# One more plain unit ahead of the block combinations, z stored raw there, filler at the mixers' seam, stores from ScalarE's queue: a two-layer decoder trunk on one core

## The chip, the core and the metric

The kernel runs on one core of a Trainium2 chip. The metric is the device time of one execution in microseconds. A measured kernel is run several times and the median counts; beside it stands one execution taken by the hardware profiler, and all rows below are from that one. Names used: TensorE (PE in the rows; PEld are its weight loads), VectorE (DVE), ScalarE (ACT), GpSimd (POOL) and SyncE (SP), which here only issues DMAs.

## The reference

Two layers over a residual stream x of 1024 tokens by 1024 channels, in float32:

```python
h = rms_norm(x, norm_pre[l])
u = h @ w_in[l]
(a_q, a_k, a_v, a_z, b_q, b_kv, b_kr, b_z, c_q, c_k, c_v, c_z, g) = jnp.split(u, split_points, axis=-1)
oa = diff_attention(...)      # 4 heads, then rms_norm per head
ob = mla_attention(...)       # 8 heads, low-rank queries and keys, rotary part
oc = sliding_window_attention(...)   # 8 heads, window 128, sinks
gates = jax.nn.sigmoid(g).reshape(B, S, N_BRANCHES, D_MODEL)
y = (gates[:, :, 0] * ((oa * jax.nn.silu(a_z)) @ w_br_a[l])
     + gates[:, :, 1] * ((ob * jax.nn.silu(b_z)) @ w_br_b[l])
     + gates[:, :, 2] * ((oc * jax.nn.silu(c_z)) @ w_br_c[l]))
x = x + rms_norm(y @ w_out[l], norm_post[l])
x = x + jax.nn.sigmoid(x @ w_ple_gate[l]) * (p[l] @ w_ple_proj[l])
```

Three attention mixers read the same normed input: a (differential), b (latent, with rotary parts), c (sliding window). Each has 512 output channels and a gate input z of the same width; silu(z) is z times its sigmoid. g holds three gates of 1024 channels, one per mixer.

## The kernel before

**Arithmetic.** Every matrix product runs on pairs: a value is split in a high part H (a rounding copy, on ScalarE) and a low part L (value minus H, on VectorE or GpSimd; `split`, lines 78 and 93), and a product is three matmuls, H·H, H·L and L·H. The normed, transposed input `hT` stays in SBUF in that form for a whole layer.

**Units.** A unit is 128 columns of u for all 1024 tokens: two halves of 512 tokens, each a `group` (line 305) of 8 K-tiles by 3 matmuls, 48 matmuls of 128x512 in all. Its weights come by one DMA (`wr`, two buffers, line 277), and are split into `wH` and `wL` (two buffers each). `z_unit` (line 434) evaluates the sigmoid of the result on ScalarE, multiplies on VectorE and stores silu(z) to the DRAM tensor `z_d`. `g_unit` (line 446) copies the result on ScalarE and stores it raw to `g_d`; its `wL` is made on GpSimd. Both use the tile `zs` (two buffers) and store from SyncE.

**Order of a layer.** `seven`, then the mixers c (`sw`), a (`da`) and b (`mla`), then `merge` and `tail`.

`seven` (line 459) first runs the four units of z for mixer a. Then VectorE makes four sets of block combinations T of `hT` (lines 479 to 500), each split again, so that `pair` (line 509) can compute two units with 7 block products in place of 8: all of z for b and c, and the first third of g. The first product of a pair goes to a bank that ScalarE copies to `p1`. The rest of g, 16 units per layer, are the **fillers**.

**Fillers.** The mixers alternate dependent steps on all engines, with TensorE waiting for softmax parts. `fill(n)` takes n steps from the front of the list of fillers; a step is 6 matmuls, and a unit is 8 of these and two steps of evacuation. In `sw` each call takes what it asks for, in `da` and `mla` a credit of 0.35 per call decides. The counts at the call sites are in `FILL`, the credits in `RATE`. `fill(n, True)` takes steps without the credit.

**Order on the engines.** The program is written in one order; a scheduler puts the instructions of each engine in a fixed order, by their place in the program, with a time model of its own. Work under `high_priority` comes earlier. `keep` pins an instruction to its place in the program.

**Trig.** In layer 0, between the two groups of 8 tiles of `sw`, `setup_trig` computes sines and cosines of the positions: some thirty small VectorE steps (lines 231 to 257), two sines on ScalarE, two transposes on TensorE (line 263), four copies and eight stores of `rope_d`, which `mla` loads into `tq`.

**Seam of da and mla.** At the end of `da` the remaining products of the last block run with filler between them; `square_sums` (line 835) sums the last squares on TensorE (line 840); then six small operations make the norm's scale out of `s0` and `ms` (lines 893 to 898). `mla` then loads its entry weight in four chunks (line 1053, tiles `wr`, split into `WH` and `WL`, 416 columns) and computes 8 tiles of 128 tokens in `mla_entry`; `rows_due` puts the transposed scale (`put_rows`, line 639) in DRAM behind the first tile. `s0` lies in the pool of `da`, whose memory the next pools take.

**Merge.** `merge` (line 1134) has to form the gated outputs: a block is 128 channels by 512 tokens. `gated` (line 1221) loads o, z and the row of scales `rb`; for mixer a VectorE multiplies o by weight and scale (line 1240) and by z (line 1241), and the result is split into `oH`, `oL`. The remaining fillers are drained meanwhile, two or so blocks per filler unit; just before the last one's matmuls the first load of `w_br_a` is written (line 277). Then come the products with `w_br_a`, 16 groups of 12 matmuls; the first needs the blocks of the first 512 tokens, the second those of the other half. For b and c GpSimd multiplies o by `rb` (line 1235), and VectorE by z (line 1243).

The list of fillers and the order of a layer are set in `build`:

```python
self.units = self.later(*[self.g_unit(l, bi, j) for bi in (1, 2) for j in range(KT)])
for b, mixer in (("c", self.sw), ("a", self.da), ("b", self.mla)):
    self.rate = RATE[b]
    mixer(l)
self.merge(l)
self.tail(l)
```

## Time and profile before

| | us |
|---|---|
| median of 3 runs | 2655.87 |
| lowest and highest | 2653.82, 2656.6 |
| the profiled execution | 2653.98 |
| its span | 2652.2 |
| TensorE busy in it | 2587.8 (98%) |
| VectorE busy | 1659.6 (63%) |
| ScalarE busy | 1265.6 (48%) |
| GpSimd busy | 452.6 (17%) |

The span goes from the first to the last instruction of the profile; the execution's own time is 1.8 us longer. The mean granted clock of TensorE over the span is 0.995 of full speed. In the rows a time stands first, then the duration, the engine, the line of the kernel, the operation with its output and inputs; the brackets hold how long the engine had been idle and what ended that.

### The profile page before, as it was taken

How to read it: one execution, taken by the hardware profiler on the slowest of the kernel's cores; microseconds unless marked ns; L12 is line 12 of the kernel's file. 1: busy time of each engine (PE TensorE's matmuls, PEld its weight loads, DVE VectorE, ACT ScalarE, POOL GpSimd, SP SyncE). 2: the span in 40 equal slices, each digit the busy share in tenths (PEclk: the TensorE clock that was granted, in tenths of full speed). 3: DMA queues.
4: the chain of work that ended last, by engine and by line, in shares of the span. 5: the costliest groups of instructions: out<-in, count | busy, mean ns of one | idle time of the engine just before them, and what ended most of it. 6: DMA issues, size and time to landing. Idle time of an engine off the chain costs nothing. (4 is left out here: it accounts for less than half of the span.)

```text
span 2652.2 us, 35930 instructions
## 1 busy us (share of the span) xinstructions
PE 2587.8 (98%) x12832; PEld 2120.4 (80%) x12832; DVE 1659.6 (63%) x3312; ACT 1265.6 (48%) x2761; POOL 452.6 (17%) x375
## 2 busy tenths in 40 slices
PE   8999999999999999999999999999999999999999
PEld 6778777888878878888877887888878788888887
DVE  7654565777378756755475536457764787577553
ACT  5433654555377733433443436545553777234332
POOL 2210000000010114234412001000000111251441
PEclk9999999999999999999999999999999999999999
DMA  6233123111110169453332331322111101894442
GB/s 197 86 116 109 46 69 104 53 52 48 51 31 23 53 210 290 148 177 115 116 96 90 114 99 50 94 68 60 51 53 40 29 22 54 267 280 148 137 118 96
DMA packets 296818, 269.21 MB, mean 102 GB/s; under 512 B 24272, under 2 KB 237456, under 8 KB 296512
## 3 DMA queue, kind: packets, MB, share of 16 engines
q1 hardware_dynamic: 295568, 262.19, 33.1%
q0 software_dynamic: 1072, 4.73, 0.6%
q8 instruction: 101, 1.65, 0.3%
q14 instruction: 77, 0.63, 0.1%
HBM read 194.93 MB, written 61.44 MB: 97 GB/s over the span
## 5 line engine op out<-in xcount | busy, mean ns | idle before, releaser
L305 PE MATMUL mm<-big,wH 128*128 128x512 f32 x3456 | 1106.5, 395 | 4.9 <-ACT zs L78 2.4
L305 PEld LDWEIGHTS mm<-big,wH 128*128 128x128 f32 x3456 | 638.9, 188 | 128.7 <-ACT zs L78 3.2
L305 PE MATMUL mm<-big,wL 128*128 128x512 f32 x1728 | 680.0, 394 | 2.3 <-POOL wL L93 1.9
L305 PEld LDWEIGHTS mm<-big,wL 128*128 128x128 f32 x1728 | 324.9, 188 | 65.7 <-POOL wL L93 2.8
L78 ACT CAST wH<-wr 128x1024 fp32r<-128x1024 f32 (+3 forms) x252 | 212.2, 852 | 334.4 <-PE mm L305 230.4
L93 DVE TENSOR_TENSOR wL<-wr,wH 128x1024 fp32r<-128x1024 f32 (+2 forms) x220 | 222.6, 1021 | 234.4 <-ACT wH L78 229.8
L793 ACT ACTIVATE e<-sc,st 128x512 f32<-128x512 f32 (+3 forms) x384 | 221.7, 582 | 99.5 <-DVE st L790 71.7
L787 DVE TENSOR_REDUCE st<-sc 128x1 f32<-128x512 f32 (+3 forms) x384 | 209.1, 551 | 7.2 <-PE sc L104 3.4
L93 POOL TENSOR_TENSOR wL<-wr,wH 128x1024 fp32r<-128x1024 f32 x32 | 77.4, 2423 | 501.7 <-ACT wH L78 336.6
L78 ACT CAST wtH<-tr 128x512 fp32r<-128x512 f32 x204 | 115.4, 590 | 82.5 <-PE tr L822 65.4
L93 DVE TENSOR_TENSOR wtL<-tr,wtH 128x512 fp32r<-128x512 f32 x204 | 136.3, 682 | 27.4 <-ACT wtH L78 26.9
L822 PE MATMUL tr<-cm,e 128*128 128x128 f32 x864 | 148.4, 275 | 1.0 <-DVE e L933 0.5
L544 PE MATMUL mm<-T,aH 128*128 128x512 f32 x384 | 121.5, 397 | 4.6 <-DVE po L583 3.9
L822 PEld LDWEIGHTS tr<-cm,e 128*128 128x128 f32 x864 | 106.1, 141 | 20.3 <-ACT e L793 7.0
L104 PE MATMUL sc<-kA,q 128*128 128x256 f32 (+3 forms) x320 | 104.6, 337 | 1.6 <-ACT e L735 0.8
L104 PE MATMUL sc<-kB,q 128*128 128x256 f32 (+3 forms) x320 | 99.6, 320 | 0.0
L544 PEld LDWEIGHTS mm<-T,aH 128*128 128x128 f32 x384 | 70.6, 188 | 26.3 <-DVE po L583 9.8
L544 PE MATMUL mm<-big,wH 128*128 128x512 f32 x256 | 82.9, 397 | 8.4 <-ACT po L78 8.4
L93 POOL TENSOR_TENSOR kL<-vT,kH 64x512 fp32r<-64x512 f32 x32 | 42.2, 1318 | 265.6 <-ACT kH L78 200.2
L379 POOL TENSOR_TENSOR acc<-acc,sq 128x512 f32<-128x512 f32 x36 | 56.8, 1577 | 176.2 <-ACT sq L378 176.2
L913 DVE TENSOR_TENSOR sc<-sc,dab 128x256 f32<-128x256 f32 (+1 forms) x128 | 52.4, 412 | 47.8 <-PE sc L104 46.6
L305 PE MATMUL mm<-WH,big 128*128 128x416 f32 x256 | 76.9, 370 | 3.6 <-ACT WH L78 2.7
(340 smaller groups left out, 5065.3 us busy)
## 6 DMA issues: line engine op xcount, KB each, us to landing
wr<-w_in SPq DMA_DIRECT2D x108, 512.0 KB, 3.8
sig<-g_d SPq DMA_DIRECT2D x48, 512.0 KB, 6.0
g_d<-zs SPq DMA_DIRECT2D x64, 256.0 KB, 2.2
wr<-w_out SPq DMA_DIRECT2D x32, 512.0 KB, 4.1
wr<-w_ple_gate SPq DMA_DIRECT2D x32, 512.0 KB, 4.0
kB<-kA SPq DMA_DIRECT2D x80, 128.0 KB, 2.3
x<-x SPq DMA_DIRECT2D x16, 512.0 KB, 6.1
g_d<-sg SPq DMA_DIRECT2D x32, 256.0 KB, 2.1
```

Source lines behind the costliest of these rows:

```text
L78: nc.scalar.copy(out, in_)
L93: (nc.vector if le == "v" else nc.gpsimd).tensor_tensor(L, src, h, ALU.subtract)
L104: self.nc.tensor.matmul(ps, w, x, start=i == 0, stop=i == n - 1)
L305: self.nc.tensor.matmul(ps, w, x, start=i == 0, stop=i == n - 1)
L379: (nc.gpsimd if eng == "g" else nc.vector).tensor_tensor(st, st, sq, ALU.add)
L544: nc.tensor.matmul(ps, w, x, start=start and not i, stop=i == 11, skip_group_check=True)
L787: nc.vector.tensor_reduce(st[:, c:c + 1], ps[:, :w], AX.X, ALU.max, negate=len(ch) == 1)
L793: nc.scalar.activation(e[:, k0:k0 + w], pss[c][:, :w], AF.Exp, bias=st[:, 0:1], accum_out=sums[:, c:c + 1])
L822: self.nc.tensor.transpose(tr[:, (2 * a + q) * P:(2 * a + q + 1) * P], ws[q][:, kt * P:(kt + 1) * P], self.ident)
L913: nc.vector.tensor_tensor(ps[:, a - k0:w], ps[:, a - k0:w], bias[:, h, a - n + 256:k0 + w - n + 256], ALU.add)
```

## The change

1. `z_unit` copies the product on ScalarE and stores raw z; no sigmoid, no multiplication. `gated` takes the sigmoid of a's z on ScalarE and multiplies it in on GpSimd, for each of the 8 blocks.
2. One unit of g (the first of the second third) runs after the four units of z in `seven`, with its low part made on VectorE; 15 units per layer are left as fillers.
3. `setup_trig` becomes a generator that stops behind the sines; what follows (transposes, copies, stores) runs ahead of the fifth tile of the second group of `sw`.
4. The stores of g units, of a's z and of a's o are issued from ScalarE's queue.
5. At the seam one filler step runs ahead of `square_sums`, its first matmul pinned; the six scale operations go into `rows_due`, which runs behind the second tile of `mla_entry`; the first filler matmul behind that place is pinned too; `s0` moves to the pool that lives through the layers.

```diff
@@ -255,6 +255,7 @@
         nc.scalar.activation(sn[:, 1], ang, AF.Sin)
         V.tensor_scalar(tr[:, 0], sn[:, 0], -MLA_SCALE, None, ALU.mult)
         V.tensor_scalar(tr[:, 1:3], sn, MLA_SCALE, None, ALU.mult)
+        yield
 
         self.cosT = self.cp.tile([P, 8, 2, 16], F32, name="cosT")
         self.sinT = self.cp.tile([P, 8, 2, 16], F32, name="sinT")
@@ -302,7 +303,10 @@
             terms += [(sH, mH), (sH, mL), (sL, mH)]
         n = len(terms)
         for i, (w, x) in enumerate(terms):
-            self.nc.tensor.matmul(ps, w, x, start=i == 0, stop=i == n - 1)
+            ins = self.nc.tensor.matmul(ps, w, x, start=i == 0, stop=i == n - 1)
+            if self.pin:
+                self.keep(ins)
+                self.pin = False
             if i % 6 == 5:
                 yield
 
@@ -435,22 +439,20 @@
         W = self.load_w(self.win(l, OFF[b + "z"] + j * P))
 
         def evac(hf, ps):
-            nc = self.nc
             st = self.zp.tile([P, 512], F32, tag="zs", bufs=2, name=self.uid("zs"))
-            nc.scalar.activation(st, ps, AF.Sigmoid)
-            nc.vector.tensor_tensor(st, ps, st, ALU.mult)
-            nc.sync.dma_start(self.z_d[l, b][j * P:(j + 1) * P, hf * 512:(hf + 1) * 512], st)
+            self.copy("a", st, ps)
+            self.nc.scalar.dma_start(self.z_d[l, b][j * P:(j + 1) * P, hf * 512:(hf + 1) * 512], st)
 
         yield from self.unit(W, KT, self.hT, evac)
 
-    def g_unit(self, l, bi, j):
-        W = self.load_w(self.win(l, OFF["g"] + bi * D + j * P), le="g")
+    def g_unit(self, l, bi, j, le="g"):
+        W = self.load_w(self.win(l, OFF["g"] + bi * D + j * P), le=le)
 
         def evac(hf, ps):
             st = self.zp.tile([P, 512], F32, tag="zs", bufs=2, name=self.uid("zs"))
             self.copy("a", st, ps)
             r0 = bi * D + j * P
-            self.nc.sync.dma_start(self.g_d[r0:r0 + P, hf * 512:(hf + 1) * 512], st)
+            self.nc.scalar.dma_start(self.g_d[r0:r0 + P, hf * 512:(hf + 1) * 512], st)
 
         yield from self.unit(W, KT, self.hT, evac)
 
@@ -461,7 +463,7 @@
         with ExitStack() as ctx:
             z = [self.z_unit(l, "a", j) for j in range(4)]
             self.by_halves(*z[0:2])
-            self.drain(*z[2:4])
+            self.drain(*z[2:4], self.g_unit(l, 1, 0, le="v"))
             pl = self.pool("seven", ctx)
             T = [[None] * 4 for _ in range(4)]
 
@@ -690,8 +692,11 @@
                     if not l:
                         self.setup_vecs()
                         self.setup_lambda(pl)
-                        self.setup_trig(pl)
+                        trig = self.setup_trig(pl)
+                        next(trig)
                 for i in range(8):
+                    if g and i == 4 and not l:
+                        next(trig, None)
                     t = self.sw_tile(l, pl, g, i, bias, sink, qs, kA[g], kB[g], Vp)
                     next(t)
                     self.fill(FILL[0])
@@ -851,7 +856,7 @@
             nc.sync.dma_start(bias, self.bias_ap(0, 4))
             heads = []
             self.diag_tiles(pl)
-            s0 = pl.tile([P, 4, 8], F32, name=self.uid("s0"))
+            s0 = self.zp.tile([P, 4, 8], F32, tag="s0", name=self.uid("s0"))
             ms = self.zp.tile([P, 4, 8], F32, tag="ms", name=self.uid("ms"))
             self.s0, self.ms = s0, ms
 
@@ -886,17 +891,24 @@
                         nxt = self.later(*prep(h + 1), front=True)
                 self.drain(*nxt)
             self.weave(late, FILL[1], True)
+            self.pin = True
+            self.fill(1, True)
             self.square_sums(self.psum("av"))
 
             f = lambda t: t.rearrange("p h i -> p (h i)")
             s0, ms = f(s0), f(ms)
-            nc.vector.reciprocal(s0, s0)
-            nc.vector.tensor_tensor(ms, ms, s0, ALU.mult)
-            nc.vector.tensor_tensor(ms, ms, s0, ALU.mult)
-            nc.scalar.activation(ms, ms, AF.Sqrt, bias=self.eps, scale=1.0 / P)
-            nc.vector.reciprocal(ms, ms)
-            nc.vector.tensor_tensor(ms, ms, s0, ALU.mult)
-            self.rows_due = lambda: self.put_rows(pl, l, "a", ms)
+
+            def scale():
+                nc.vector.reciprocal(s0, s0)
+                nc.vector.tensor_tensor(ms, ms, s0, ALU.mult)
+                nc.vector.tensor_tensor(ms, ms, s0, ALU.mult)
+                nc.scalar.activation(ms, ms, AF.Sqrt, bias=self.eps, scale=1.0 / P)
+                nc.vector.reciprocal(ms, ms)
+                nc.vector.tensor_tensor(ms, ms, s0, ALU.mult)
+                self.put_rows(pl, l, "a", ms)
+
+            self.rows_due = scale
+            self.pin = True
             self.fill(FILL[6], True)
 
     def da_block(self, l, pl, h, b, t, bias, late):
@@ -948,7 +960,7 @@
             sq = pl.tile([P, 256], F32, tag="sq", bufs=2, name=self.uid("sq"))
             nc.scalar.activation(sq, av[:, :256], AF.Square)
             self.squares = sq, self.ms[:, h, 2 * b:2 * b + 2]
-            nc.sync.dma_start(self.o_d[l, "a"][h * P:(h + 1) * P, b * 256:(b + 1) * 256], o)
+            nc.scalar.dma_start(self.o_d[l, "a"][h * P:(h + 1) * P, b * 256:(b + 1) * 256], o)
 
         return rest()
 
@@ -1063,7 +1075,7 @@
                 self.weave(self.group(ps[:, :N], KT,
                                       lambda kt: tuple(x[:, sl] for x in self.hT[hf][kt]),
                                       lambda kt: (WH[:, kt], WL[:, kt])), 1, not hf and t < 2)
-                if self.rows_due:
+                if self.rows_due and t:
                     self.rows_due()
                     self.rows_due = None
                 r = p2.tile([P, 512], F32, tag="raw", bufs=5, name=self.uid("raw"))
@@ -1231,7 +1243,11 @@
                 rb[a * P // ns:(a + 1) * P // ns],
                 rd[j * ns + a:j * ns + a + 1, src[1]].to_broadcast([P // ns, 512]))
         nc.sync.dma_start(z, self.z_d[l, b][src])
-        if b != "a":
+        if b == "a":
+            sg = pl.tile([P, 512], F32, tag="sg", bufs=2, name=self.uid("sg"))
+            nc.scalar.activation(sg, z, AF.Sigmoid)
+            nc.gpsimd.tensor_tensor(z, sg, z, ALU.mult)
+        else:
             nc.gpsimd.tensor_tensor(o, o, rb, ALU.mult)
         yield
         if b not in og:
@@ -1357,13 +1373,14 @@
         self.setup()
         self.fillers, self.squares = [], None
         self.credit, self.rate, self.units = 0.0, 1.0, ()
+        self.pin, self.rows_due = False, None
         with self.ent:
             self.entry()
             self.setup_bias(self.pe)
         self.zp = self.pool("zst")
         for l in range(DEPTH):
             self.seven(l)
-            self.units = self.later(*[self.g_unit(l, bi, j) for bi in (1, 2) for j in range(KT)])
+            self.units = self.later(*[self.g_unit(l, n // KT, n % KT) for n in range(KT + 1, 3 * KT)])
             for b, mixer in (("c", self.sw), ("a", self.da), ("b", self.mla)):
                 self.rate = RATE[b]
                 mixer(l)
```

## Rows read from the trace of the kernel before

**Rows 1.** The page's first part: busy time, share of the span, instructions.

```profile
PE 2587.8 (98%) x12832; PEld 2120.4 (80%) x12832; DVE 1659.6 (63%) x3312; ACT 1265.6 (48%) x2761; POOL 452.6 (17%) x375
```

**Rows 2.** Waits of TensorE: waiting line, releaser, total us, times, longest us.

```profile
PE mm L544 <- ACT po L78: 8.4, 2, 7.5
PE mm L305 <- ACT zs L78: 4.4, 6, 1.2
PE tr L263 <- ACT sincos L252: 4.2, 1, 4.2
...
PE mm L305 <- ACT WH L78: 2.7, 2, 2.0
PE tr L639 <- DVE ms L898: 2.2, 1, 2.2
```

**Rows 3.** Windows: length, busy time (instructions) by engine, PE clock, DMA share, GB/s.

```profile
core 0: us, PE busy (x) PEld busy (x) DVE busy (x) ACT busy (x) POOL busy (x), PEclk, DMA share, GB/s
349.00:362.00 13.00, 8.85 (x39) 7.47 (x38) 9.49 (x37) 2.96 (x6) 0.00 (x0) 0.74 0.16 44
660.00:700.00 40.00, 36.77 (x183) 32.21 (x182) 14.35 (x29) 12.86 (x27) 5.67 (x3) 0.96 0.27 82
1389.00:1402.00 13.00, 5.53 (x18) 4.12 (x17) 11.64 (x20) 5.13 (x9) 0.00 (x0) 0.74 0.15 40
1970.00:2005.00 35.00, 30.42 (x146) 25.41 (x145) 16.11 (x30) 13.97 (x29) 5.66 (x3) 0.90 0.29 86
2258.80:2302.00 43.20, 43.20 (x193) 35.68 (x191) 23.87 (x29) 12.41 (x20) 9.46 (x5) 1.00 0.85 278
```

**Rows 4.** Timeline of TensorE at layer 1's first pair.

```profile
1397.02 1.22 PE L544 MATMUL mm<-big,wH 128*128 128x512 f32 x2 [7.47 <-ACT po L78]
...
1401.41 0.63 PE L544 MATMUL mm<-T,aH 128*128 128x512 f32 x2
```

**Rows 5.** Timeline of ScalarE at the same place.

```profile
1395.86 0.62 ACT L78 CAST T<-po 128x512 fp32r<-128x512 f32 x1 [4.35 <-DVE po L500]
1396.39 0.58 ACT L78 COPY po<-mm 128x512 f32<-128x512 f32 x1
```

**Rows 6.** Tile zs: its instructions, ns min/median/max, first and last start.

```profile
L453 SPq DMA_DIRECT2D g_d<-zs x64: 319/338/1365, 321.4 to 2305.8; - x64
L440 ACT ACTIVATE zs<-mm x16: 583/592/600, 32.8 to 1381.7; 128x512 f32<-128x512 f32 x16
L441 DVE TENSOR_TENSOR zs<-mm,zs x16: 678/682/691, 33.5 to 1383.5; 128x512 f32<-128x512 f32 x16
```

**Rows 7.** Timeline of ScalarE and SyncE at layer 0's seam.

```profile
667.76 1.68 ACT L78 CAST WH<-wr 128x832 fp32r<-128x832 f32 x2 [0.77 <-DVE ms L898]
...
670.65 0.34 SPq L453 DMA_DIRECT2D g_d<-zs  x1
...
672.04 0.91 SPq L1053 DMA_DIRECT2D wr<-w_in  x2
...
675.75 0.89 ACT L78 CAST WH<-wr 128x832 fp32r<-128x832 f32 x1 [5.12 <-DMA wr<-w_in]
```

**Rows 8.** Timeline of layer 1's merge prelude: SyncE, GpSimd and VectorE.

```profile
2260.30 0.39 SPq L277 DMA_DIRECT2D wr<-w_in  x1
...
2270.76 2.55 POOL L93 TENSOR_TENSOR wL<-wr,wH 128x1024 fp32r<-128x1024 f32 x1 [10.49 <-ACT wH L78]
2271.09 2.77 DVE L1241 TENSOR_TENSOR o<-o,z 128x512 f32<-128x512 f32 x1
...
2293.23 0.69 DVE L93 TENSOR_TENSOR oL<-o,oH 128x512 fp32r<-128x512 f32 x1 [0.69 <-ACT oH L78]
...
2293.66 0.39 SPq L277 DMA_DIRECT2D wr<-w_br_a  x1
...
2300.83 1.23 DVE L93 TENSOR_TENSOR wL<-wr,wH 128x1024 fp32r<-128x1024 f32 x1 [3.59 <-ACT wH L78]
```

**Rows 9.** GpSimd's multiplication in the pairs, ns min/median/max, first and last start.

```profile
L557 POOL TENSOR_TENSOR sg<-po,sg x32: 1284/1294/1695, 82.2 to 1472.2; 128x512 f32<-128x512 f32 x32
```

## The prediction, made before the change was run

> **What bounds the kernel now.** I read the page's busy table first: TensorE is busy 98% of the span [rows 1]. So only its gaps can be won, and the next view is the list of what TensorE waited for [rows 2]. Five entries there belong to places that the change touches: 8.4 us for the copy of p1 in the block combinations, 4.4 for the copies of z and g, 4.2 for the sine table, 2.7 for the chunks of the latent mixer's weight, 2.2 for the scale of the differential mixer. They make 21.9 us. The rest of what TensorE loses there doesn't show as waiting: after a gap the granted clock is low. The table of windows puts it at 0.74 around the trig gap and around layer 1's combinations, 0.96 and 0.90 at the two seams between the mixers [rows 3]. One minus the clock, times the length, gives 3.4, 3.4, 1.6 and 3.5 us, but part of that lies in the gap itself, so these are upper bounds. The timeline shows the rest of it: two matmuls take 1.22 us at 1397.02 and 0.63 us at 1401.41 [rows 4], 1.2 GHz against 2.4 GHz.
>
> The last window to read is the prelude of the merge, 2258.8 to 2302.0: TensorE has no gap there [rows 3], because four filler units cover what VectorE does. That cover is what the change spends.
>
> **Sum base.** Durations are those of the profiled execution: 2653.98 us, span 2652.2 and 1.8 around it. The median of the three runs, 2655.87, stands 1.9 above, so what I add up is taken off the median. Some 0.2%, 5.3 us, is what a measurement of this kernel can tell from no change.
>
> **A. A fifth unit ahead of the combinations, z stored raw.** In layer 1 TensorE ends its work at 1389.55 and waits 7.47 us for p1's copy on ScalarE [rows 4]. That copy stands behind a split of T, which itself waited 4.35 us for VectorE [rows 5]: VectorE's chain of combinations is late, and ScalarE's queue is in order. A unit is 48 matmuls; the prelude runs 193 in 43.2 us, 0.224 each [rows 3], so a unit covers 10.7 us. Eight multiplications of z per layer leave VectorE at 0.68 us each, 5.4 us [rows 6]; the unit's own wL split comes to VectorE at about 1.2, as that of w_br_a at 2300.83 does [rows 8]. Cover grows by 10.7, VectorE's load shrinks by some 4: the 7.47 goes whole, and so does its slow stretch, at most 3.4, of which I take 1.5. Layer 0 has only 8.4 − 7.47 = 0.9 us of this wait; I take it whole. That is 9.9, and **A = −9**, since a wait may come up at a later product of the pair; bounds −6 and −12. What is late next: the pair's products that take the splits of T in order.
>
> **B. The trig tail moves behind four tiles of the second group.** TensorE's transpose waits 4.2 us for the sine [rows 2], because VectorE works through the angle's many small steps first: it is busy 9.49 of that window's 13 us, in 37 instructions [rows 3]. Later transposes and filler come ahead of it now. Removed: 4.15 plus a slow stretch of at most 3.4, of which I take 2.6. But those 9.5 us of VectorE stay in front of the tiles' maxima, and only about 6 us of matmuls (two tiles' score products, transposes, three filler steps) can run meanwhile; so I take **B = −5** of the 6.75, bounds 0 and −6.75. The eight stores of rope_d move too, on SP, by four tiles; their reader is the latent mixer, whose weights in layer 0 are loaded at 672 [rows 7], 300 us later, so they cost nothing.
>
> **C. The seam, both layers.** Layer 1: 2.21 for the scale and 0.67 for the chunk, layer 0: 2.0 for the chunk [rows 2]; 4.9 us. The pinned filler step (6 matmuls, 1.4 us) stands where TensorE idled; the chain of six scale operations leaves the seam, and runs behind the second tile of the entry. Moving s0 to the longer-lived pool frees the memory of the mixer without waiting for the chain: in layer 0 the first cast of WH starts at 667.76, released by that chain [rows 7]. Slow stretches: at most 1.6 and 3.5, I take 1.4 and 2.1. Sum 4.9 + 3.5 = 8.4, **C = −8**, bounds −2 and −10. The new delay is that the rows' store goes out some 5 us later; its reader is the merge, whose blocks stand at 2271 in layer 1 [rows 8], over 260 us on: no cost.
>
> **D. Stores issued from ScalarE.** 112 stores leave SP: 64 of g, 16 of z, 32 of o. In layer 0's seam SP holds a store of g until its copy is done (670.65), and the loads of the last two chunks, written behind it, go at 672.04; their cast starts at 675.75 after 5.12 us of waiting [rows 7]. With the store on ScalarE's queue the loads can leave up to 2 us earlier; that is inside C. Elsewhere the z waits of 4.4 us lose their multiplication (0.68 of a chain of 0.59 + 0.68 [rows 6]) and one store's turn: **D = −1**, bounds 0 and −4.4.
>
> By the Trainium skill, "DMA: Bandwidth & Descriptors", section "Issuing engines are not separate DMA queues", DMAs begun from different engines share the same 16 DMA engines, and beginning them elsewhere saves only the sequencer's time. By that the chunk's 2.0 us at layer 0's seam would stay, and the sum would be 2 us worse. The order on SP [rows 7] is my reason not to take it: what is saved there is the turn behind a waiting store, not the issue.
>
> **E. What ScalarE pays.** No row has a DMA issued by ScalarE. Nearest: SP takes 0.34 us for one [rows 6]. 112 × 0.34 = 38 us of ScalarE's time, which is busy 48% of the span [rows 1]. Below: nothing, since a store follows a copy on the same engine (a gain is counted in D). Above: in the differential mixer (32 stores of o) ScalarE feeds the exponentials; if every one of those came late by 0.34, 11 us. The store also makes ScalarE's queue wait for nothing new: the copy ahead of it is its own. I take **E = +2**, nearer the lower end because TensorE's waits for ScalarE in that mixer are too short to stand among the first rows [rows 2].
>
> **F. The merge's prelude.** One unit fewer is left for it: cover falls from 43.2 to 32.5 us in layer 1. Needed by then: w_br_a's wL and the eight gated blocks, the second group of products (12 matmuls, 2.7 us in) needing the last four. Now the eighth block's oL ends at 2293.92, 35.1 after the mixer [rows 8]. w_br_a's load went out at 2293.66, and its wL ended at 2302.06, just as TensorE arrived [rows 8]. The load of the last filler unit, though, went out at 2260.30 [rows 8], as soon as its slot fell free: with one unit fewer w_br_a is that tile, and I expect it out there. The blocks: z now passes ScalarE (0.59 [rows 6]) and GpSimd (1.29 per multiplication [rows 9]) ahead of VectorE's o·z: 2 us at the start, and while GpSimd multiplies, VectorE's two-operand work stands, as it did for 2.77 in place of 0.69 beside the split at 2270.76 [rows 8]. Part of it falls in the 0.7 us that VectorE waits for each oH anyway; one filler split fewer on GpSimd gives back 2.1. So the eighth block at about 38 to 41 against 35 needed: **F = +4 per layer, +8**; bounds 0 and +15 per layer.
>
> **Sum.** −9 − 5 − 8 − 1 + 2 + 8 = −13: own time 2641.0, against the median **2642.9**, say 2643.
>
> **Rivals.**
> 1. *The merge starves (slower).* If w_br_a's load stays behind the blocks' loads on SP, as at 2293.66, all 10.7 us of lost cover per layer are stall, and blocks held by GpSimd add up to 8 × 1.29 = 10.3 less 2.1; I take 4. That is 15 per layer, 30 in all, in place of 8: −21 + 30 = +9, 2665. It decides from the point where the load leaves later than some 24 us after the mixer (33 less 8.4 for landing, cast and split). For it: the wL ended within 0.1 us of its use. Against: the slot falls free earlier.
> By the Trainium skill, "SBUF — State Buffer", section "SBUF: two separate sides", VectorE and GpSimd share one port pair as an exclusive lock held for the whole instruction. The rows agree (2.77 beside 2.55), and by the rule each of the 8 multiplications could hold VectorE fully.
> 2. *The gaps at trig and seams are only replaced*, VectorE's backlog and the chunks' landing being what they are: B 0, C −2, A −9, D 0, E +2, F +4 gives −5, about 2651, between 2649 and 2657.
> 3. *The change doesn't do what it says.* Only the first matmul of a filler step is pinned; a scheduler orders the rest by its own clock, and may pull the moved work back to where it was: with A partly filled and F paid, within 2651 to 2661.
> 4. *More than that*: F and E hidden, all gaps and slow stretches gone: −31 near the lower bounds, 2624.
>
> **Numbers.** Forecast (2630 to 2650) 0.57; more 0.10; replaced 0.13, of which 0.04 still faster by over 0.2%; not done 0.05; starved 0.15, of which 0.03 within 0.2%. Faster 0.57 + 0.10 + 0.04 = 0.71; same 0.09 + 0.05 + 0.03 = 0.17; slower 0.12. The range 2630 to 2660 leaves out the 0.10 below and about as much of the starved case.
>
> **What would show it.** A: no TensorE gap over 1 us at the first pair of layer 1, clock 1.00 there. B: no wait of L263's transposes, and waits of the scores for VectorE of no more than 2 us behind it. C: filler matmuls between the mixer's last products and the square sums; the scale chain after the second entry tile. D: loads of chunks leaving SP without a store between. E: no TensorE wait for ScalarE's exponentials that was not there. F: the first product with oH some 33 to 38 us after the mixer's end, and w_br_a's load before the blocks' loads. The prediction is wrong if TensorE stands over 10 us in either prelude, or if the seven's wait returns at a later pair.

## The result, and the profile after

The changed kernel takes 2669.78 us (median of 6 runs), the kernel before 2654.16 beside it: ratio 1.0055, 95% interval 1.0042 to 1.0068. It is 15.6 us slower, where 13 us faster was forecast. The profiled execution took 2670.93 us, its span is 2669.1. The page's busy times (the lines of the changed kernel lie up to 16 further down):

```profile
PE 2594.1 (97%) x12832; PEld 2127.3 (80%) x12832; DVE 1669.5 (63%) x3298; ACT 1279.3 (48%) x2779; POOL 470.4 (18%) x389
```

TensorE runs the same 12832 matmuls in 6.3 us more than before and stands 10.6 us longer; together these are the 16.9 us by which the span grew.

What TensorE waited for, total us, times, longest us:

```profile
PE mm L306 <- ACT zs L78: 10.9, 7, 2.9
PE sc L306 <- ACT oH L78: 5.2, 2, 2.8
PE mm L306 <- DVE wL L93: 4.7, 5, 2.1
PE sc L104 <- ACT e L798: 3.6, 5, 1.7
PE mm L306 <- ACT WH L78: 3.1, 2, 1.6
PE av L104 <- ACT wtH L78: 2.8, 3, 2.4
...
PE tr L641 <- DVE ms L907: 1.1, 2, 0.6
```

Against [rows 2], the waits for p1 (8.4) and for the sines (4.2) are gone, and that for the scale is half. In their place TensorE waits 10.9 us for the fillers' copies, 5.2 for gated blocks (`oH`), and the chunks (`WH`) cost 3.1, not less than before. The windows at the places of [rows 3], where each now lies:

```profile
335.00:348.00 13.00, 10.56 (x49) 8.64 (x48) 6.39 (x30) 6.87 (x24) 3.53 (x4) 0.87 0.48 94
660.00:700.00 40.00, 35.93 (x158) 29.85 (x158) 14.85 (x25) 13.19 (x25) 5.63 (x3) 0.83 0.27 82
1406.00:1419.00 13.00, 13.00 (x59) 10.76 (x58) 7.65 (x10) 6.68 (x10) 1.50 (x1) 1.00 0.20 61
1985.00:2020.00 35.00, 29.21 (x131) 23.21 (x130) 13.83 (x21) 12.31 (x21) 5.66 (x3) 0.85 0.29 86
957.30:1000.50 43.20, 35.62 (x144) 27.59 (x141) 29.08 (x28) 15.92 (x26) 15.30 (x11) 0.91 0.74 244
2277.50:2320.70 43.20, 38.30 (x164) 30.93 (x163) 25.37 (x27) 15.81 (x26) 15.96 (x12) 0.96 0.78 255
```

Layer 1's first pair runs without a gap at clock 1.00 (0.74 before). The trig part now costs a shorter gap (one wait of 2.4 us, clock 0.87). But the seams' clock went down, from 0.96 and 0.90 to 0.83 and 0.85, and in the 43.2 us after the latent mixer, where TensorE had one gap of 1.2 us in layer 0 and none in layer 1, it now idles 7.6 and 4.9 us.

Where the 16.9 us of span came from, by stretches between TensorE instructions that both traces have (last product with T; last sum of squares; last product with `WH`; transposition of the latent mixer's sums; last product with `og`, the gated blocks of mixer b, so that "merge" here ends with the products of b), in us:

| stretch | layer 0 before, after | layer 1 before, after |
|---|---|---|
| z units and pairs | 225.9, 230.3 | 469.9, 468.8 (with layer 0's tail) |
| mixers c and a | 439.9, 437.5 | 436.9, 434.6 |
| entry of the latent mixer | 61.0, 67.1 | 61.9, 66.8 |
| latent mixer | 215.9, 222.3 | 214.7, 217.2 |
| merge | 132.8, 132.9 | 131.3, 131.2 |
| tail | | 262.1, 260.5 |

The first row holds one more unit (10.7 us) in each layer, so it gained 6 in layer 0 and 12 in layer 1. The merge holds one unit less and takes as long as before: what was moved out of it, 10.7 us per layer, was lost there. The entry lost 11 us, where C had a gain of 8, and the mixer behind it 9, which no step of the prediction has (layer 0's holds 14 more matmuls than before, some 3 us of filler).

### The profile page after: what moved, and what is told of

Its sections match the earlier page's. It is cut to its first block, busy times and chain, and to the rows that moved or that the text cites. A ratio compares the mean times of both kernels' runs of the same rounds, so it can differ in the third digit from the quotient of the medians.

```text
span 2669.1 us, 35887 instructions
## 1 busy us (share of the span) xinstructions
PE 2594.1 (97%) x12832; PEld 2127.3 (80%) x12832; DVE 1669.5 (63%) x3298; ACT 1279.3 (48%) x2779; POOL 470.4 (18%) x389
## 4 chain that ended last, share of the span: by engine, by line
PE 82%; DVE 5%; DMA 5%; ACT 4%; issue 2%; SPq 1%; POOL 1%; ACTq 0%; DVEq 0%; POOLq 0%
PE mm L306 46%; PE sc L104 8%; PE mm L546 7%; PE av L811 5%; PE sc L306 4%; PE tr L827 3%; PE sc L546 2%; PE tr L306 2%; DMA wr<-w_in 2%; DMA wr<-w_br_b 1%; DVE wL L93 1%; ACT wH L78 1%; PE tr L748 1%; DVE o L1256 1%; ACT e L740 1%
## 5 line engine op out<-in xcount | busy, mean ns | idle before, releaser
L306 PE MATMUL mm<-big,wH 128*128 128x512 f32 x3456 | 1112.8, 397 | 10.6 <-ACT zs L78 8.0
L559 POOL TENSOR_TENSOR sg<-po,sg 128x512 f32<-128x512 f32 x32 | 44.6, 1393 | 215.5 <-ACT sg L557 215.5
```

The source lines that it names most:

```text
L306: ins = self.nc.tensor.matmul(ps, w, x, start=i == 0, stop=i == n - 1)
L559: nc.gpsimd.tensor_tensor(sg, src, sg, ALU.mult)
```

## The experiments

All ratios are to the kernel before on the same chip, with 95% intervals; 0.1% is 2.7 us.

**First four: one part undone in the changed kernel.** Silu back in the seven, and no sigmoid or GpSimd multiplication in the merge:

```diff
-            self.copy("a", st, ps)
+            nc.scalar.activation(st, ps, AF.Sigmoid)
+            nc.vector.tensor_tensor(st, ps, st, ALU.mult)
...
-        if b == "a":
-            sg = pl.tile([P, 512], F32, tag="sg", bufs=2, name=self.uid("sg"))
-            nc.scalar.activation(sg, z, AF.Sigmoid)
-            nc.gpsimd.tensor_tensor(z, sg, z, ALU.mult)
-        else:
+        if b != "a":
```

> The changed kernel with part 1 undone: z of the differential mixer gets its sigmoid and multiplication in the seven again, the merge does neither; the fifth unit, the seam, the trig split and ScalarE's stores stay. Theory M (the merge starves: GpSimd's eight multiplications stretch VectorE's chain of blocks, and one unit of cover is gone): the blocks' cadence goes back from 4.0 to 2.8 us, the eighth is done some 10 us earlier, and 15 to 25 of the 27 us lost in the merge come back: 2645 to 2655. Theory Q (ScalarE's queue, jammed by the stores it issues, makes the loss): within 4 us of the changed kernel, 2666 to 2674. Theory S (the seam with the moved scale chain makes it): the same, 2666 to 2674.

Measured: 1.0012 (1.0001 to 1.0023), 11 us faster than the changed kernel, less than theory M has and more than Q and S. The seven kept most of its gain (no wait for p1; its two stretches are 1.6 and 0.9 us longer), so with the unit ahead, raw z buys little there. Layer 1's merge fell to 122.7 us; in layer 0 it stayed at 131.3, now waiting for the casts of w_br_a's later loads.

The 112 stores back on SyncE (`nc.scalar.dma_start` to `nc.sync.dma_start` for g, z and o):

> The changed kernel with the 112 stores issued by SyncE again, all else as changed. Theory Q: the entry of the latent mixer and the mixer itself lost 17 us over both layers because casts and copies stand behind stores on ScalarE; most of it comes back, 2652 to 2660. Theory M: nothing in the merge depends on it, 2666 to 2674. Theory S: the entry's loss stays, 2666 to 2674; the chunk loads wait behind a store again, up to 2 us worse.

Measured: 1.0086 (1.0070 to 1.0101), 8 us slower still, which none of the three theories has. The entries took 71.5 and 68.6 us. Theory Q falls here: among the other parts, ScalarE's stores helped.

The seam as before:

```diff
-            self.pin = True
-            self.fill(1, True)
...
-            self.rows_due = scale
-            self.pin = True
...
-            s0 = self.zp.tile([P, 4, 8], F32, tag="s0", name=self.uid("s0"))
+            s0 = pl.tile([P, 4, 8], F32, name=self.uid("s0"))
```

> The changed kernel with the seam as before: no filler step ahead of the square sums, no pins, the scale chain at once, s0 in the mixer's own pool. Theory S: the entry took 10.5 us more in both layers together because the transposed scale stands in the middle of the first tiles and holds TensorE and the chunk casts; that comes back and the old gaps of 4.9 with it: 2661 to 2666. Theories M and Q: the seam had gained what was planned and the entry lost for other reasons, so undoing it costs 3 to 8 us: 2672 to 2678.

Measured: 1.0026 (1.0017 to 1.0035), 8 us faster. The entries went back to 61.3 and 63.1 us, as theory S has it: the seam, planned as a gain of 8, was a loss.

16 fillers and no fifth unit, z still raw:

```diff
-            self.drain(*z[2:4], self.g_unit(l, 1, 0, le="v"))
+            self.drain(*z[2:4])
...
-            self.units = self.later(*[self.g_unit(l, n // KT, n % KT) for n in range(KT + 1, 3 * KT)])
+            self.units = self.later(*[self.g_unit(l, n // KT, n % KT) for n in range(KT, 3 * KT)])
```

> The changed kernel with 16 filler units again and no fifth unit ahead of the combinations; z stays raw there and the merge's GpSimd multiplies. Theory M, cover part: TensorE has 10.7 us more per layer to run in the merge's prelude, so 15 to 21 us come back there; plain z alone must hold the seven's wait: if VectorE's 5.4 us are enough, the wait of 7.5 falls to 2, else it stays; 2650 to 2660. Theories Q and S: the merge's loss has nothing to do with cover; 2666 to 2676.

Measured: 1.0097 (1.0082 to 1.0112), 11 us slower than the changed kernel. The merges took 137.1 and 140.8 us: with a whole unit more to run, TensorE stood for the fillers' own copies (7.1 and 6.6 us). So what the merge lacks there is not cover. In layer 1 the wait for p1 fell from 7.5 to 2.3 us with raw z alone.

**Second four: pairs of parts.** The first run has units and z as before, the second also the seam, the third adds the unit to the second; the fourth is the changed kernel with the six scale operations in place and only `put_rows` deferred, behind the first tile.

> The changed kernel with the fifth unit and the raw z both undone (16 filler units, silu in the seven); trig split, seam and ScalarE's stores stay. Theory M2 (the merge takes the time that its blocks, weights and transfers need, some 131 us from the mixer's end to its last product, with or without the unit; each half alone left a loss there of 21 to 23 us of stalls against 4 before): with both undone the merge loses under 6 us in both layers together, the seven's wait of 7.5 is back, the seam's loss of some 6 stays: 0 to 5 us above the kernel before. Theory Q2 (the stores on ScalarE hold up casts in the merge): the stalls of 10 us or more in the merge stay without the multiplications, 8 to 20 us above the kernel before.

> The kernel before with only the trig split and the stores from ScalarE. Theory M2 with S: these two are the parts that gain outside the merge: trig 5, the stores some 2 to 5 at the seams; 4 to 10 us below the kernel before. Theory Q2: the stores cost 5 or more in the merge, so no better than the kernel before, minus 2 to plus 6.

> As the run with the trig split and the stores alone, with the fifth unit ahead of the combinations added (silu made in the seven, merge without sigmoid and multiplication, seam as before). Theory M2: the unit gains some 12 us in the seven and gives back what the merge cannot shorten by, 2 to 11 of it per layer: between 8 below and 2 above the run without it. Theory C (cover is what the merge lacks): all 10.7 per layer come back as stalls, 5 to 12 above the run without it.

> The changed kernel with the scale chain made at once, its rows behind the first tile, while the filler step, the pins and the longer-lived s0 stay. Theory S1 (the deferred chain is what costs: its table load and square root stand between the chunk casts on ScalarE, and its transposition holds TensorE in the entry's second tile): the stretch from the square sums to the end of the entry falls from 67 to 61 to 63 us, 5 to 10 us faster than the changed kernel. Theory S2 (the filler's place is what costs: fewer steps stand between the square sums and the first tile, so TensorE meets the chunks before they are there): the stretch stays at 66 to 68 us, within 4 us of the changed kernel.

Measured: 1.0070 (1.0052 to 1.0088), 1.0040 (1.0024 to 1.0056), 0.9997 (0.9988 to 1.0007), 1.0065 (1.0049 to 1.0081). The first has the size of theory Q2 and not its place: its merges took 127.8 and 134.5 us, the longer stretches are above all the entries and the latent mixers. The second was to be faster and is 11 us slower, so trig and stores by themselves hold a loss. The unit takes off 11 us beside them, more than either theory has. The fourth kept the entries at 67.7 us in both layers: making the scale late is not what costs (S1 falls).

**Third four: parts alone on the kernel before.**

> The kernel before with only the trig split. Theory P (parts add up): the sliding-window mixer of layer 0 loses 5 us less, as in every run with the split, and nothing else moves: 3 to 7 us below the kernel before. Theory R (any moved work shifts the fixed order and the fillers behind it, so a part's gain in its own stage is given back in later ones): the same 5 us less in its stage, but 3 to 10 us more in the latent mixer, the merge and the second layer: between 2 below and 6 above the kernel before.

> The kernel before with only the 112 stores issued from ScalarE. Theory Q3 (the stores jam ScalarE where the fillers' copies stand behind them): the excess of 10 us that the trig split and the stores had together belongs to the stores: 8 to 14 us above the kernel before, with waits of TensorE for the copy zs in both preludes. Theory P with the changed kernel's own result, where going back to SyncE made it 8 us slower: 4 to 10 us below the kernel before.

> The kernel before with only the fifth unit ahead of the combinations (silu made as before, 15 filler units). Theory M2: the seven gains some 14 us in both layers together and the merge gives back 3 to 14: 0 to 11 us below the kernel before. Theory C (cover is what the merge lacks): the merge gives back 21, so 5 to 10 above.

> The kernel before with the trig split and the fifth unit, no raw z, stores from SyncE, seam as before. Theory P: the two single gains add, 5 to 14 us below the kernel before. Theory R: they don't, within 4 us of the better of the two alone; the merge's stalls differ by 5 or more from those of the run with the unit alone, though nothing in the merge was changed between the two.

Measured: trig 0.9979 (0.9970 to 0.9989); stores 1.0046 (1.0031 to 1.0061); unit 0.9999 (0.9990 to 1.0008); trig and unit 0.9973 (0.9964 to 0.9982). Trig is the forecast 5 us, and parts add up there: in the trace no other stretch moved by more than 1 us. The unit alone gains in the seven and gives it back in the merge (128.3 and 131.7 us with a unit less).

With trig and unit the merges take 128.9 and 127.9 us, so of the 21.4 us that left them 14 are lost, with no raw z in the kernel. SyncE, ScalarE and TensorE in its first prelude, where the mixer ended at 943.5:

```profile
981.59 0.32 SPq L457 DMA_DIRECT2D g_d<-zs  x1
982.01 0.38 SPq L278 DMA_DIRECT2D wr<-w_br_a  x1
...
988.28 1.04 ACT L78 CAST wH<-wr 128x1024 fp32r<-128x1024 f32 x1 [6.71 <-DMA wr<-w_br_a]
...
989.37 0.64 PE L306 MATMUL sc<-oH,wH 128*128 128x512 f32 x1 [2.25 <-ACT wH L78]
```

The blocks were ready and the first load of `w_br_a` had left at 945.00. But the products now begin 12 us earlier, and the second load stands on SyncE behind the last filler's store, which waits for that filler's copy. With the stores on ScalarE as well (the run at 0.9997) the second load leaves at 980.25, 33.4 us after the mixer in place of 38.5, and layer 0's merge takes 122.2 us, the whole unit less; layer 1's, at 129.1, then waits 3.8 us for the third load's cast.

The stores alone lose 12 us. TensorE in the second prelude of the run with the stores alone:

```profile
2307.54 0.72 PE L305 MATMUL mm<-big,wH 128*128 128x512 f32 x2 [0.92 <-ACT zs L78]
```

and ScalarE at the same place:

```profile
2303.62 0.62 ACT L78 CAST oH<-o 128x512 fp32r<-128x512 f32 x1 [2.79 <-DVE o L1244]
2306.39 0.62 ACT L78 CAST oH<-o 128x512 fp32r<-128x512 f32 x1 [2.15 <-DVE o L1244]
2306.91 0.58 ACT L78 COPY zs<-mm 128x512 f32<-128x512 f32 x1
2307.52 0.33 ACTq L456 DMA_DIRECT2D g_d<-zs  x1
```

The copy that frees TensorE's bank stands behind a cast that waits 2.15 us for VectorE. In the kernel before, copies stand behind casts too, but TensorE met none of them late there: it was busy for all of its 43.2 us [rows 3]. The issue itself takes 0.33 us. Such waits make 5 us in the two preludes; the longest growth, 9.7 us, is that of layer 1's latent mixer (224.4 us against 214.7), which was not followed to a cause.

With these the change can be built up link by link: before 1; trig 0.9979; unit 0.9973; stores 0.9997; seam 1.0012; raw z 1.0055, the changed kernel. In us, of 2655: −5.6, −1.6, +6.4, +4.0, +11.4. For the second and the fourth the intervals of the two runs overlap.

**Fourth four: inside the links.** The first is trig and unit with `RATE` 0.29 in place of 0.35 for a and b; the second the changed kernel with `nc.vector.tensor_tensor(z, sg, z, ALU.mult)`; the third pins each of the four steps behind the square sums; the fourth is the kernel before with the stores of z and o alone on ScalarE.

> The kernel before with the trig split and the fifth unit, as in the fastest run so far, and the fillers' credit in the differential and the latent mixer at 0.29 in place of 0.35, which leaves the merge its 44 steps again as it had with 16 units. Theory C (cover is what the merge lacks when a unit is moved): the merge's excess falls from 9.7 and 8.6 us to under 3 in each layer, and the mixers, which use 5 steps fewer each, lose less than that: 5 to 15 us below the run with the two parts alone (ratio 0.992 to 0.995). Theory E (the mixers need those steps): their stretches lose the same, ratio 0.996 to 1.000.

> The changed kernel with the eight multiplications of the sigmoid into z made on VectorE in place of GpSimd. Theory L (GpSimd's multiplication holds VectorE's two-operand work, which stretches a block from 2.8 to 4 us): VectorE does 0.7 us more per block and isn't held, so the blocks come at 3.3 to 3.6 us and the preludes' excess falls by 3 to 8 us in all: ratio 1.002 to 1.004. Theory O (ScalarE's order of sigmoid, casts and copies is what stretches it): the cadence stays at 4 us and the ratio at 1.004 to 1.007.

> The changed kernel with each of the four filler steps behind the square sums pinned, not only the first. Theory S2 (TensorE meets the entry's first tile after two steps where it had four before, and stands in front of the chunks): with all four ahead of the tile, the stretch from the square sums to the entry's end falls from 67 to 61 to 63 us in both layers and its low clock goes: ratio 1.000 to 1.003. Theory S3 (it is the longer life of s0 or the chunks' transfers): the stretch stays at 66 or more, ratio 1.004 to 1.007.

> The kernel before with only the stores of z and of o issued from ScalarE, those of g from SyncE as before. Theory G (the stores of g are what cost: they put the fillers' copies at other places in ScalarE's order, so TensorE waits for zs in the preludes and the latent mixer): the 12 us of all three together fall to 0 to 3. Theory N (any store on ScalarE's queue costs its 0.33 us where the differential mixer needs the exponentials): 4 to 10 us above the kernel before.

Measured: 0.9971 (0.9960 to 0.9983), no different from 0.9973, in the range of E and outside that of C: TensorE's waits in the merges shrink by 3 us each, and layer 1's latent mixer takes 3.4 us longer. 1.0022 (1.0012 to 1.0031): 9 of raw z's 11 us come back with the same work on VectorE, in the range of L and outside that of O. 1.0089 (1.0073 to 1.0104): more pins, more loss, against S2. 1.0009 (1.0000 to 1.0018): the stores of g are the ones that cost. VectorE in layer 0's prelude, in the changed kernel, with GpSimd beside it:

```profile
972.27 2.99 POOL L1249 TENSOR_TENSOR z<-sg,z 128x512 f32<-128x512 f32 x2 [1.81 <-ACT sg L1248]
972.30 1.81 DVE L1256 SCALAR_TENSOR_TENSOR o<-o,sub,rb 128x512 f32<-128x512 f32 x1
974.22 1.59 DVE L1257 TENSOR_TENSOR o<-o,z 128x512 f32<-128x512 f32 x1
...
976.50 0.69 DVE L93 TENSOR_TENSOR oL<-o,oH 128x512 fp32r<-128x512 f32 x1 [0.69 <-ACT oH L78]
977.08 1.29 POOL L1249 TENSOR_TENSOR z<-sg,z 128x512 f32<-128x512 f32 x1 [1.82 <-ACT sg L1248]
977.11 1.80 DVE L1256 SCALAR_TENSOR_TENSOR o<-o,sub,rb 128x512 f32<-128x512 f32 x1
```

and with the multiplication on VectorE:

```profile
972.83 0.74 DVE L1256 SCALAR_TENSOR_TENSOR o<-o,sub,rb 128x512 f32<-128x512 f32 x1
973.49 0.68 DVE L93 TENSOR_TENSOR oL<-o,oH 128x512 fp32r<-128x512 f32 x1
974.10 0.68 DVE L1257 TENSOR_TENSOR o<-o,z 128x512 f32<-128x512 f32 x1
974.70 0.68 DVE L1249 TENSOR_TENSOR z<-sg,z 128x512 f32<-128x512 f32 x1
975.30 0.74 DVE L1256 SCALAR_TENSOR_TENSOR o<-o,sub,rb 128x512 f32<-128x512 f32 x1
```

An operation of 0.74 takes 1.80 beside GpSimd's 1.29. Blocks come every 3.7 to 4.8 us, 4.2 in the mean. Before they came every 2.8, with two stops of 4.8, 3.4 in the mean; on VectorE alone, with one operation more, every 2.5, with two stops of 5.0, 3.2 in the mean. By the Trainium skill, "SBUF — State Buffer", section "SBUF: two separate sides", whichever of a GpSimd operation and a VectorE one with two SBUF inputs starts first holds the shared ports for the whole instruction. The rows agree: GpSimd starts at 977.08, VectorE at 977.11, and VectorE takes 1.80.

**Last two: the seam's halves** on trig and unit (0.9973). First the filler step and the pins only, then the deferred chain and s0 only:

```diff
+            self.pin = True
+            self.fill(1, True)
             self.square_sums(self.psum("av"))
...
+            self.pin = True
             self.fill(FILL[6], True)
```

> The kernel before with the trig split and the fifth unit (ratio 0.9973), and of the seam only the filler step ahead of the square sums and the two pins; the scale chain at once, s0 in the mixer's pool, all stores from SyncE. Theory K (the pins cost: a pinned step takes the filler out of the scheduler's hands where it had filled the entry's waits): the stretch from the square sums to the entry's end rises by 2 to 5 us per layer, ratio 0.999 to 1.001. Theory D (the deferred chain and s0 cost): no change or a gain of up to 4, ratio 0.996 to 0.998.

```diff
+            s0 = self.zp.tile([P, 4, 8], F32, tag="s0", name=self.uid("s0"))
...
+            self.rows_due = scale
...
+                if self.rows_due and t:
```

> The same base (0.9973) with only the other half of the seam: the scale chain behind the entry's second tile and s0 in the longer-lived pool; no step ahead of the square sums, no pins. Theory D: the transposed scale and the table load fall between the chunks, the stretch rises by 2 to 5 us per layer, ratio 0.999 to 1.001. Theory K: the wait of 2.2 for the scale in layer 1 goes and nothing comes in its place, ratio 0.995 to 0.998.

Measured: pins 1.0055 (1.0041 to 1.0069), deferral **0.9951** (0.9939 to 0.9964). The step and its two pins cost 0.8%, some 22 us (18 between the profiled executions); the deferral gains 6, and that kernel, at 2643.4 us against 2656.5, is the fastest of all. Its interval just touches that of the base. From square sums to the entry's end the two take 70.5 and 70.3, and 59.4 and 60.2 us (base 61.1 and 63.3); the mixer behind it 219.4 and 218.2 with pins, 215.9 and 216.6 with the deferral (base 215.9 and 215.0). Layer 0's seam in the base, on SyncE, ScalarE and TensorE:

```profile
671.41 0.34 SPq L457 DMA_DIRECT2D g_d<-zs  x1
...
672.79 1.99 SPq L1060 DMA_DIRECT2D wr<-w_in  x2
...
676.65 0.88 ACT L78 CAST WH<-wr 128x832 fp32r<-128x832 f32 x1 [5.27 <-DMA wr<-w_in]
...
677.59 0.65 PE L306 MATMUL mm<-WH,big 128*128 128x416 f32 x2 [2.16 <-ACT WH L78]
```

With the pins, on SyncE:

```profile
670.43 0.32 SPq L457 DMA_DIRECT2D g_d<-zs  x1
...
672.50 0.33 SPq L457 DMA_DIRECT2D g_d<-zs  x1
672.88 1.35 SPq L981 DMA_DIRECT2D tq<-rope_d  x3
674.33 0.92 SPq L1063 DMA_DIRECT2D wr<-w_in  x2
```

on ScalarE:

```profile
669.82 0.59 ACT L78 COPY zs<-mm 128x512 f32<-128x512 f32 x1 [0.52 <-PE mm L306]
670.31 0.89 ACT L78 CAST WH<-wr 128x832 fp32r<-128x832 f32 x1
671.89 0.58 ACT L78 COPY zs<-mm 128x512 f32<-128x512 f32 x1 [0.70 <-PE mm L306]
672.37 0.89 ACT L78 CAST WH<-wr 128x832 fp32r<-128x832 f32 x1
677.87 0.89 ACT L78 CAST WH<-wr 128x832 fp32r<-128x832 f32 x1 [4.61 <-DMA wr<-w_in]
```

on TensorE:

```profile
678.81 0.71 PE L306 MATMUL mm<-WH,big 128*128 128x416 f32 x1 [3.00 <-ACT WH L78]
```

and the windows of both seams:

```profile
660.00:700.00 40.00, 33.89 (x151) 28.07 (x150) 12.25 (x24) 12.63 (x23) 5.70 (x3) 0.83 0.28 82
1985.00:2020.00 35.00, 26.46 (x110) 21.49 (x111) 9.16 (x19) 11.39 (x20) 5.70 (x3) 0.85 0.30 86
```

The same with the deferral only, SyncE:

```profile
667.41 0.40 SPq L1064 DMA_DIRECT2D wr<-w_in  x1
...
672.79 0.39 SPq L1064 DMA_DIRECT2D wr<-w_in  x1
```

ScalarE:

```profile
665.43 1.68 ACT L78 CAST WH<-wr 128x832 fp32r<-128x832 f32 x2 [0.74 <-ACT sq L960]
667.13 1.28 ACT L905 ACT_TABLE_LOAD   x1
```

and both windows:

```profile
660.00:700.00 40.00, 36.84 (x191) 32.27 (x189) 13.57 (x33) 13.16 (x30) 5.69 (x3) 1.00 0.29 82
1985.00:2020.00 35.00, 31.60 (x158) 27.59 (x158) 15.49 (x37) 10.85 (x34) 4.73 (x2) 1.00 0.10 29
```

With the pins two filler halves are evacuated inside the seam; in the base it is one. Their copies stand before and between the first chunk casts, and their stores before the loads of the last two chunks. (Layer 1 has both copies before the casts.) Counted from the square sums (666.5 in the base, 668.0 here), the second chunk's cast starts 1.5 us later; the last loads leave as late as in the base, 6.3 us. In layer 1 the first cast starts 0.3 and the loads leave 0.8 us later. TensorE's waits in the stretch grow by more: from 3.4 to 7.3 us, and in layer 1 from 5.8 to 7.8. One minus the clock, times the length, grows from 1.7 to 6.8 and from 3.4 to 5.1; in layer 1 12 more filler matmuls fall there as well. With the deferral the casts start at 665.43, ahead of the scale's table load, and a third chunk's load leaves at 667.41. Its waits in the stretch are 3.2 and 5.6 us, hardly less than in the base; the clock is 1.00 in both layers, against 0.97 and 0.95.

## Why the prediction was wrong

**A** held in its place: both waits for p1 went, and the first row of the table gained 18 in both layers together where 9 were forecast. **B** was right in sign and size (−5, measured −5.6). But A spends a unit of the merge, and F was to price that.

**F** is the first failing term: forecast +8, measured 21, since merges with 10.7 us less to run took as long as before. In the changed kernel TensorE waits there for blocks and for the fillers' copies. "Part of it falls in the 0.7 us that VectorE waits for each oH anyway" put the eighth block 38 to 41 us after the mixer; it came at 44.9 (1002.2 less 957.3) and 44.7. The hold falls on VectorE's next operation, not on its wait: the multiplication starts when the sigmoid is done, just as VectorE takes the next block. Raw z costs 11.4 us as the last link, 9 of them by GpSimd. The sign of being wrong that the prediction set here, over 10 us of standing in a prelude, did not come (7.6 and 4.9): layer 0's merge has 8.5 us of low clock on top.

F would have failed without raw z too. It followed w_br_a's first load, which went out early (949.28 in layer 0), as forecast, and stopped there. With trig and unit alone the products begin earlier, the next load is late, behind a filler's store, and 14 us are lost in the merges. Rival 1 named the right place and sign and gave w_br_a's first load as the main cause; in the changed kernel TensorE waits for no load of w_br_a in the preludes. With the unit alone it waits for the second one, so the kind of cause was right there.

**C** is the second: forecast −8, a loss of 4 to 8. The half that was argued from the trace, the chain, gains 6 with s0. The half that was taken for granted, "The pinned filler step (6 matmuls, 1.4 us) stands where TensorE idled", costs 22 alone. TensorE's waits in the entry did not shrink with it, they grew by 3.9 and 2.0 us, and the low clock behind them takes 5.1 and 1.7 us more. I had counted the step's matmuls and not the copy and the store that come with it; the rows show these among the chunks' casts and loads. That they are the whole cause is not shown: they delay the chunks by less than the waits grew, and a step moved ahead of the square sums is also missing behind them. No run has the step without the pins or the pins without the step. The run with the scale at once parts s0's longer life from the deferred chain only beside the pins, where the two kernels differ within their intervals.

**D and E**, forecast +1 together: alone they cost 12, as a link 6, and undone in the changed kernel 8 more is lost. The sign set for E failed, though not in the mixer that it was argued for: TensorE's waits for the exponentials went from 0.8 to 3.6 us, all of the growth in the latent mixer. The issue time (0.33 each) is the smaller part, since the 48 stores of z and o cost 2 us and the 64 of g the rest; the places in ScalarE's fixed order would explain that, and these differ with each neighbour. My reason was the turn on SyncE: the load at 672.04 of [rows 7] did leave at 670.13, and the entry still got longer. By the Trainium skill, "DMA: Bandwidth & Descriptors", section "Issuing engines are not separate DMA queues", only the sequencer's time is saved. At the seam that stood nearer; in layer 0's merge, beside the unit, a load left 5 us earlier and the turn was worth more. Why the sign turns with company is settled no further than that; nor why the pins lengthen the latent mixer by 3 us too, 60 us behind them, which is shown but not explained.

## What to carry to other kernels

A filler is not only matmuls: its evacuation copy and its store take places in in-order queues, and a step that is moved takes them along. Before moving work out of a stage, ask what the stage waits for next once that work is gone: this merge took 131 to 133 us before, and with a unit less anything from 122 to 133. When a change has several parts, time each alone: here trig gained alone, half of the seam gained, and the unit gained nothing alone but 11 us beside the stores.

## What the runs showed of the hardware

In these traces the granted clock does not go by the sum of the waits alone. In layer 0's seam the kernel with the deferral only waited 0.56, 1.20, 0.65 and 0.74 us, 3.2 in all, at clock 1.00. Before, the one wait of 2.0 among them (3.2 in all, too) was followed by matmuls at 1.2 GHz and a window of 0.96; with the pins, waits of 1.30 and 3.00, among 6.1 in all, gave 0.83. Layer 1, from the square sums to the entry's end, agrees: 5.6 us of waits at 1.00 with the deferral, 5.3 at 0.945 before. One minus the clock, over layer 0's window, is 6.8 us lost with the pins against none, more than the 2.9 us by which the waits differ.
